# Gathered expert rows in a diffusion trunk: first gathers placed among the gate-matrix builds, selections reordered

## The chip, the core and the metric

The kernel runs on one core of a Trainium2 chip. The metric is the device time of one launch in microseconds (us). A profiled execution gives a trace; its span is the time from the first to the last instruction.

The engines: PE is TensorE (matrix multiplication), DVE is VectorE, ACT is ScalarE, POOL is GpSimd (here it issues the gathers), SP issues most other transfers. Each engine works through a queue of its own, in order.

## The reference

Two layers of a trunk; the part that matters here is the channel mixer of each layer, a lookup of single-neuron experts. 640 tokens (128 of a context, 512 of a sample) choose 8 x 16 of 16384 experts each.

```python
def peer_ffn(h, wq, k1, k2, u, v):
    q = (xt @ wq).reshape(n, PEER_HEADS, PEER_DKEY)
    s1 = jnp.einsum('thd,hnd->thn', q[..., :half], k1)
    s2 = jnp.einsum('thd,hnd->thn', q[..., half:], k2)
    v1, i1 = lax.top_k(s1, PEER_TOPK)
    v2, i2 = lax.top_k(s2, PEER_TOPK)
    cand = v1[..., :, None] + v2[..., None, :]
    cidx = i1[..., :, None] * PEER_NKEYS + i2[..., None, :]
    top, pos = lax.top_k(cand.reshape(...), PEER_TOPK)
    idx = jnp.take_along_axis(cidx.reshape(...), pos, axis=-1)
    g = jax.nn.softmax(top, axis=-1)
    ...
    act = jax.nn.gelu(jnp.einsum('td,thkd->thk', xc, u[ic]))
    w = gc * act
    return jnp.einsum('thk,thkd->td', w, v[ic])
```

## The kernel before

A layer is `mix` (projections, linear attention, convolution, neighbourhood attention) and then `peer`, which the change touches. `peer` splits the 640 tokens into five tiles of 128, numbered 0 to 4, and computes them in two ways.

**Tiles 0 and 1: gathered.** For each of 128 slots (8 heads x 16 experts) POOL fetches one row of `uv` per token, 128 x 2048 floats, 1 MB in one indirect transfer. `gather(t, s0)` does two slots, and `pump()` takes the next such pair from the list `todo`, 128 pairs in all for a layer: two gathers, two dot products with the token's activations on DVE (L754), a gelu on ACT (L756), a product with the gate (L757), and two accumulations on DVE (L763). `uv` has four buffers (`NUV`), two pumps' worth.

**Tiles 2 to 4: dense.** All 16384 experts are run through PE for these 384 tokens in 128 blocks of 128 experts, and a gate matrix that is zero for experts not chosen masks the result. `dense(b)` loads 512 KB of `uT` and 512 KB of `uv` on SP's queue into the four `raw` buffers, splits each into a high and a low part (ACT L836, DVE L837), runs 24 matmuls into `ps_a` (L857 to L859), a gelu (ACT L861), the product with the gate block `gres` (DVE L862), a split of that (L869, L870) and 18 matmuls into `acc` (L877). The loop over `b` calls one pump in each block, tied behind the gate product of the block before (`tc.issue_after`).

**The gate matrix.** `build(i)` makes the gate matrix for 16 dense tokens at a time, 24 builds in all, eight per tile: one-hot matrices of the two halves of the expert index (DVE L782, L784, from `ixT`), scaled by the gates (ACT L788, from `gT`), a matmul per token into `ps_g` (PE L791), and evictions by ACT (L793, L799) and DVE (L797) to `gres` and `sg`; `sg` then goes to HBM (`gsp`, L802) and comes back in dense, block group by block group (L846).

**Selections.** `level1` takes the best 16 of 128 keys for two heads of a tile. `select(t)` combines them for tile t: candidates, the best 16 of 50, softmax (Exp on ACT, L675), index lookup by masks (L702). For tiles 0 and 1 it ends in `gidx` (L715), for the others in `ixT` and `gT`. It is nearly all DVE. Tiles 1 to 4 pass `level1` while the queries are projected; tile 0 passes it in step `l0`.

**Order.** `select(2)` comes first, then the steps of `ORDER`: `b2` is the eight builds of tile 2, `s3` is `select(3)`, `l0` is `level1` of tile 0, and so on. `select(1)` stands in the dense loop at block `BSEL` = 16. A planner lays out every engine's queue when the program is built: of the instructions that it takes to be ready, the one earliest in the program goes first, so that later work fills gaps.

In layer 0 the builds also call `ada_steps` (`NADA` = 2 steps for 8 tokens): the modulation of the next layer, 256 KB loads of `w_ada` into `NWA` buffers and two matmuls each (L162). The same buffers serve the first modulation at the kernel's start.

**Memory.** `kp` is a pool that lives from the projection of the queries to the end of the builds and holds `kk` (keys), `qd` and others. The pools of dense (`raw`, `u`, `v`) open after it has closed, in its place.

Of the kernel before, what the change touches and what calls it, by code (L numbers as in the profile page):

```python
# [10 lines left out]
F32 = mybir.dt.float32  # L11
# [4 lines left out]
BF16 = mybir.dt.bfloat16  # L16
F16 = mybir.dt.float16
AF = mybir.ActivationFunctionType
OP = mybir.AluOpType
# [3 lines left out]
D = 1024  # L23
# [21 lines left out]
TD = T - TG  # L45
# [7 lines left out]
NUV = 4  # L53
# [6 lines left out]
ORDER = "b2 s3 b3 s4 l0 b4 s0".split()  # L60
BSEL = 16
ADA1 = 4
NWA = 4
# [6 lines left out]
class Trunk:  # L70
    def __init__(self, ctx, tc, I, O):
# [3 lines left out]
        V, S = self.V, self.S  # L75
# [16 lines left out]
        self.iota8 = consts.tile([128, 128, 8], BF16, name="iota8")  # L92
# [12 lines left out]
        V.tensor_copy(self.iota8, self.iota[:, :, None].to_broadcast([128, 128, 8]))  # L105
# [466 lines left out]
    def peer(self, l):  # L572
# [10 lines left out]
        ixT = gat.tile([128, 2, TD], BF16, name="ixT")  # L583
        gT = gat.tile([128, TD], F32, name="gT")
# [8 lines left out]
        kp = self.pool(f2, f"tk{l}", 1)  # L593
        f1 = ExitStack()
# [15 lines left out]
        def level1(units):  # L610
            ps = psb.tile([128, 2, 2, 128], F32, name="ps_k", tag="k")
            s2 = kp.tile([128, 2, 2, 128], F32, name="s2", tag="s2", bufs=3)
# [123 lines left out]
        gres = gpool.tile([128, NR, NTC, GB, TC], F32, name="gres")  # L736
        bp = self.pool(f2, f"gb{l}", 2)
        self.wp = bp

        ga = {}  # L740

        def gather(t, s0, n=2):
            if s0 == 0:
                ga["acc"] = gat.tile([128, D], F32, name="gacc", tag="gacc", bufs=1)
                ga["dots"] = gat.tile([128, 128], F32, name="dots", tag="dots")
                ga["w"] = gat.tile([128, 128], F32, name="gw", tag="gw")
# [20 lines left out]
        todo = [(t, s) for t in range(2) for s in range(0, 128, 2)]  # L767

        def pump(n=1):
            for _ in range(n):  # L770
                if todo:
                    gather(*todo.pop(0))
# [3 lines left out]
        def build(tcn):  # L776
            sg = bp.tile([128, NSP, GB, TC], F32, name="sg", tag="sg")
            for t8 in range(0, TC, 8):
# [5 lines left out]
                V.tensor_tensor(ohq, ixT[:, 1, None, t0:t0 + 8].to_broadcast([128, 128, 8]), self.iota8, op=OP.is_equal)  # L784
# [15 lines left out]
                for _ in range(NADA):  # L800
                    next(ada, None)
            nc.sync.dma_start(gsp[:, :, tcn].rearrange("r p b t -> p r (b t)"), sg.rearrange("p r b t -> p r (b t)"))  # L802
# [11 lines left out]
        select(2)  # L814
# [6 lines left out]
        gb = self.pool(st, f"gu{l}", NUV, side="right")  # L821
# [69 lines left out]
        for b in range(128):  # L891
            dense(b)
            if b == BSEL:
                select(1)
            with tc.issue_after(gates[max(0, b - GLAG)]):
                while todo and left - len(todo) < left * (b + 1) / 128:
                    pump()
# [111 lines left out]
```

## Time and profile before

| | |
|---|---|
| median of three runs | 4156.69 us (4152.92 to 4169.66) |
| span of the profiled execution | 4144.4 us |
| PE busy in it | 3810.6 us (92%) |
| DVE busy | 3333.9 us (80%) |
| ACT busy | 1701.2 us (41%) |
| POOL busy | 757.7 us (18%) |
| moved by DMA | 1011.89 MB, mean 244 GB/s |
| build stretch, layer 0 and 1 | 708 to 958 us, 2723 to 2948 us |
| dense stretch, layer 0 and 1 | 968.6 to 2098 us, 2957 to 4090 us |

A build stretch is counted from the first one-hot to the last eviction, a dense stretch from the first gelu (layer 0) or just ahead of the first blocks (layer 1) to the last block. Busy shares are averages over stages that have different limits, so the stretches say more than the whole span. Matmuls overlap and their ends are modelled, so a busy PE is not a PE at its peak.

### The profile page before, as it was taken

The page shows a single profiled execution, that of the slowest core. Times are in us where ns is not written, and L with a number is a line of the kernel's source. Part 1 is how long each engine was busy: PE and PEld are TensorE (multiplying, and loading weights), DVE is VectorE, ACT ScalarE, POOL GpSimd, SP SyncE. Part 2 cuts the span into 40 slices and gives each one's busy share as a digit, 9 for nine tenths or more (in the row PEclk, how much of TensorE's full clock was granted, in tenths as well). Part 3 has the DMA queues.
Part 4 walks back from the last instruction along what each step waited for, and adds up shares of the span by engine and source line. Part 5 has one row for each costly group of instructions (what it writes and reads, how often), then busy time and mean ns, then how long its engine had stood idle before and what let it go on. Part 6 is the DMA issues. An engine that isn't in the chain of part 4 may idle for free.

```text
span 4144.4 us, 54329 instructions
## 1 busy us (share of the span) xinstructions
PE 3810.6 (92%) x19884; PEld 3204.7 (77%) x19884; DVE 3333.9 (80%) x6618; ACT 1701.2 (41%) x3268; POOL 757.7 (18%) x532
## 2 busy tenths in 40 slices
PE   7999997888999999999989999867799999999998
PEld 4896775557888888888878988745688888888886
DVE  4762359788999999999968633988799999999997
ACT  4423332884333333333354243368633333333333
POOL 0000000002333333333300000000133333333331
PEclk8999998998999999999999999978899999999999
DMA  4124232668999999999921221023599999999995
GB/s 161 33 61 128 74 110 68 186 202 291 382 367 387 373 377 375 377 376 379 375 90 33 62 69 57 26 68 113 205 355 383 375 375 372 377 377 377 381 375 213
DMA packets 302267, 1011.89 MB, mean 244 GB/s; under 512 B 28273, under 2 KB 116721, under 8 KB 236209
## 3 DMA queue, kind: packets, MB, share of 16 engines
q0 software_dynamic: 73728, 536.90, 33.5%
q1 hardware_dynamic: 210560, 425.45, 29.4%
q10 hardware_dynamic: 17712, 46.07, 2.8%
q8 instruction: 156, 2.56, 0.2%
q14 instruction: 111, 0.90, 0.1%
HBM read 960.49 MB, written 47.84 MB: 243 GB/s over the span
## 4 chain that ended last, share of the span: by engine, by line
issue 37%; PE 29%; POOL 13%; ACT 9%; DVE 7%; DMA 5%; POOLq 0%; ACTq 0%; DVEq 0%; SPq 0%
PE ps_pj L235 13%; POOL uv L751 13%; ACT qg L788 5%; DMA uv<-uv,gidx 4%; PE ps_ada L162 2%; PE ps_lv L363 2%; PE ps_g L791 2%; PE acc L877 1%; PE npo L529 1%; ACT sg L799 1%; PE ps_s L508 1%; PE ps_ms L187 1%; ACT nt L208 1%; PE po L421 1%; PE pt L524 1%
## 5 line engine op out<-in xcount | busy, mean ns | idle before, releaser
L751 POOL DMA_INDIRECT uv<-uv,gidx x512 | 750.5, 1466 | 3317.0 <-PE ps_g L791 1766.2
L754 DVE SCALAR_TENSOR_TENSOR uv<-uv,ht 128x1024 f32<-128x1024 f32 x512 | 624.2, 1221 | 116.2 <-DMA uv<-uv,gidx 115.4
L859 PE MATMUL ps_a<-hd,ulo 128*128 128x384 f32 x2048 | 695.2, 339 | 17.8 <-DVE ulo L837 17.8
L857 PE MATMUL ps_a<-hd,uhi 128*128 128x384 f32 x2048 | 700.7, 342 | 9.6 <-ACT uhi L836 9.6
L858 PE MATMUL ps_a<-hd,uhi 128*128 128x384 f32 x2048 | 694.0, 339 | 0.0
L763 DVE SCALAR_TENSOR_TENSOR gacc<-uv,gw,gacc 128x1024 f32<-128x1024 f32 x508 | 652.5, 1284 | 15.7
L877 PE MATMUL acc<-vhi,whi 128*128 128x512 f32 x1536 | 506.2, 411 | 67.1 <-ACT whi L869 66.4
L877 PE MATMUL acc<-vhi,wlo 128*128 128x512 f32 x1536 | 486.9, 398 | 2.0 <-DVE wlo L870 1.7
L836 ACT ACTIVATE vhi<-raw 128x1024 fp32r<-128x1024 f32 x256 | 271.6, 1061 | 511.7 <-PE acc L877 496.1
L877 PE MATMUL acc<-vlo,whi 128*128 128x512 f32 x1536 | 480.0, 394 | 0.0
L859 PEld LDWEIGHTS ps_a<-hd,ulo 128*128 128x128 f32 x2048 | 388.3, 190 | 24.9 <-DVE ulo L837 22.7
L857 PEld LDWEIGHTS ps_a<-hd,uhi 128*128 128x128 f32 x2048 | 387.8, 189 | 21.2 <-ACT uhi L836 10.8
L877 PEld LDWEIGHTS acc<-vhi,whi 128*128 128x128 f32 x1536 | 271.6, 189 | 160.4 <-ACT whi L869 113.1
L858 PEld LDWEIGHTS ps_a<-hd,uhi 128*128 128x128 f32 x2048 | 387.7, 189 | 10.0
L788 ACT ACTIVATE qg<-ohq,gT 128x128 f32<-128x128 bf16 x768 | 341.3, 533 | 59.5 <-DVE ohq L784 59.5
L791 PE MATMUL ps_g<-ohp,qg 128*128 128x128 f32 x1536 | 297.9, 338 | 69.5 <-ACT qg L788 68.9
L791 PEld LDWEIGHTS ps_g<-ohp,qg 128*128 128x128 f32 x1536 | 238.4, 221 | 151.9 <-ACT qg L788 116.0
L877 PEld LDWEIGHTS acc<-vhi,wlo 128*128 128x128 f32 x1536 | 282.1, 189 | 81.7 <-DVE wlo L870 24.9
L877 PEld LDWEIGHTS acc<-vlo,whi 128*128 128x128 f32 x1536 | 290.3, 189 | 65.7
L837 DVE TENSOR_TENSOR vlo<-raw,vhi 128x1024 fp32r<-128x1024 f32 x256 | 312.1, 1219 | 13.5 <-ACT vhi L836 13.3
L756 ACT ACTIVATE gw<-dots 128x2 f32<-128x2 f32 x256 | 52.1, 203 | 646.6 <-DVE uv L754 646.4
L837 DVE TENSOR_TENSOR ulo<-raw,uhi 128x1024 fp32r<-128x1024 f32 x256 | 312.8, 1222 | 0.0
(243 smaller groups left out, 6187.5 us busy)
## 6 DMA issues: line engine op xcount, KB each, us to landing
raw<-uT SPq DMA_DIRECT2D x256, 512.0 KB, 6.4
raw<-uv SPq DMA_DIRECT2D x256, 512.0 KB, 8.4
wada<-w_ada SPq DMA_DIRECT2D x192, 256.0 KB, 3.3
gsp<-sg SPq DMA_DIRECT2D x48, 896.0 KB, 5.0
gres<-gsp ACTq DMA_DIRECT2D x112, 384.0 KB, 14.5
wraw<-w_in SPq DMA_DIRECT2D x56, 512.0 KB, 3.6
wraw<-w_out SPq DMA_DIRECT2D x16, 512.0 KB, 3.6
wraw<-wq SPq DMA_DIRECT2D x16, 512.0 KB, 4.0
```

The lines of the kernel that those rows point to most:

```text
L235: self.PE.matmul(ps[j][:, :n], w[:, k, :], x[:, k, :], start=(k == 0 and i == 0), stop=(k == 7 and i == 2))
L751: G.indirect_dma_start(out=b, out_offset=None, in_=I["uv"], in_offset=bass.IndirectOffsetOnAxis(ap=gidx[t][:, s:s + 1], axis=0))
L754: V.scalar_tensor_tensor(b[:, :D], b[:, :D], 1.0, ht[t], op0=OP.mult, op1=OP.mult, accum_out=dots[:, s:s + 1])
L763: V.scalar_tensor_tensor(acc_, b[:, D:], w[:, s:s + 1], acc_, op0=OP.mult, op1=OP.add)
L788: S.activation(qg[:, t, :], ohq[:, :, t4 + t], AF.Copy, scale=gT[:, t0 + t4 + t:t0 + t4 + t + 1])
L791: PE.matmul(ps[:, t, :], qg[:, t, :], ohp[:, t4 + t, :], start=True, stop=True)
L836: S.activation(hi, raw, AF.Copy)
L837: V.tensor_tensor(lo, raw, hi.bitcast(F32), op=OP.subtract)
L857: PE.matmul(ps, uhi[:, ks], hd[0][:, k, :], start=(k == 0), stop=False)
L858: PE.matmul(ps, uhi[:, ks], hd[1][:, k, :], start=False, stop=False)
L859: PE.matmul(ps, ulo[:, ks], hd[0][:, k, :], start=False, stop=(k == 7))
L877: PE.matmul(acc[:, t, j, :], a[:, ts], x[:, j * 512:(j + 1) * 512], start=(b == 0 and i == 0), stop=(b == 127 and i == len(parts) - 1))
```

## The change

The first 12 pumps of each layer move from dense into the builds, one after every second build (`EARLY` = 2), and work on tile 1, whose selection moves ahead of the builds; `todo` runs tile 1 first. `select(0)` takes the place of `select(1)` in dense. Dense spreads the remaining 116 pumps over its 128 blocks. To have the memory, `NWA` goes from 4 to 3, `s2` from three buffers to two, the pools of the gathers open ahead of the builds, `ixT` and `gT` move into `kp`, and `iota8` is made once in each layer, not kept.

```diff
-ORDER = "b2 s3 b3 s4 l0 b4 s0".split()
+ORDER = "s2 s1 b2 s3 b3 s4 l0 b4".split()
+EARLY = 2
-NWA = 4
+NWA = 3
...
-        self.iota8 = consts.tile([128, 128, 8], BF16, name="iota8")
-        V.tensor_copy(self.iota8, self.iota[:, :, None].to_broadcast([128, 128, 8]))
...
-        ixT = gat.tile([128, 2, TD], BF16, name="ixT")
-        gT = gat.tile([128, TD], F32, name="gT")
...
         kp = self.pool(f2, f"tk{l}", 1)
+        ixT = kp.tile([128, 2, TD], BF16, name="ixT")
+        gT = kp.tile([128, TD], F32, name="gT")
...
-            s2 = kp.tile([128, 2, 2, 128], F32, name="s2", tag="s2", bufs=3)
+            s2 = kp.tile([128, 2, 2, 128], F32, name="s2", tag="s2", bufs=2)
...
+        gx = self.pool(st, f"gx{l}", side="right")
+        gb = self.pool(st, f"gu{l}", NUV, side="right")
         bp = self.pool(f2, f"gb{l}", 2)
+        iota8 = bp.tile([128, 128, 8], BF16, name="iota8", tag="iota8", bufs=1)
+        V.tensor_copy(iota8, self.iota[:, :, None].to_broadcast([128, 128, 8]))
...
-                ga["acc"] = gat.tile([128, D], F32, name="gacc", tag="gacc", bufs=1)
-                ga["dots"] = gat.tile([128, 128], F32, name="dots", tag="dots")
-                ga["w"] = gat.tile([128, 128], F32, name="gw", tag="gw")
+                ga["acc"] = gx.tile([128, D], F32, name="gacc", tag="gacc")
+                ga["dots"] = gx.tile([128, 128], F32, name="dots", tag="dots")
+                ga["w"] = gx.tile([128, 128], F32, name="gw", tag="gw")
...
-        todo = [(t, s) for t in range(2) for s in range(0, 128, 2)]
+        todo = [(t, s) for t in (1, 0) for s in range(0, 128, 2)]
...
+            if tcn % EARLY == EARLY - 1:
+                pump()
             nc.sync.dma_start(gsp[:, :, tcn].rearrange("r p b t -> p r (b t)"), sg.rearrange("p r b t -> p r (b t)"))
...
-        select(2)
         for c in ORDER:
...
-        gb = self.pool(st, f"gu{l}", NUV, side="right")
...
             if b == BSEL:
-                select(1)
+                select(0)
```

## Rows read from the trace of the kernel before

**Rows 1.** Windows: us; busy us PE, PEld, DVE, ACT, POOL; clock, DMA, GB/s.

```profile
708.00:958.00 250.00, 213.82 (x1022) 131.57 (x1022) 199.75 (x613) 211.92 (x567) 4.63 (x4) 0.88 0.62 190
...
968.60:2098.00 1129.40, 1090.10 (x5345) 957.40 (x5344) 1048.98 (x1414) 398.47 (x636) 372.93 (x258) 1.00 0.96 370
...
2723.00:2948.00 225.00, 174.10 (x782) 130.12 (x782) 188.20 (x568) 204.43 (x555) 2.82 (x3) 0.86 0.35 106
...
2957.00:4090.00 1133.00, 1084.91 (x5285) 952.95 (x5284) 1045.74 (x1414) 398.97 (x633) 371.57 (x252) 0.99 0.96 369
```

**Rows 2.** Windows, middle of layer 0's dense stretch.

```profile
1100.00:2000.00 900.00, 868.19 (x4251) 761.82 (x4250) 834.59 (x1122) 318.30 (x506) 299.93 (x202) 1.00 0.98 377
```

**Rows 3.** First row: the gelu's line, 1100 to 2000. Others: timeline (start, length).

```profile
L861 ACT ACTIVATE w<-ps_a x101: 468/492/496, 1103.2 to 1994.1; 128x384 f32<-128x384 f32 x101
...
2062.88 0.49 ACT L861 ACTIVATE w<-ps_a 128x384 f32<-128x384 f32 x1 [1.04 <-PE ps_a L859]
...
2071.35 0.49 ACT L861 ACTIVATE w<-ps_a 128x384 f32<-128x384 f32 x1 [1.04 <-PE ps_a L859]
```

**Rows 4.** Waits of DVE, 1100 to 2000: us in total, times, longest.

```profile
DVE uv L754 <- DMA uv<-uv,gidx: 46.5, 39, 3.0
```

**Rows 5.** DMA view, 1100 to 2000: slices; issues, KB, us to landing.

```profile
GB/s 389 376 357 376 392 368 343 400 376 369 406 359 362 406 363 371 399 376 355 401 370 375 374 388 353 374 390 371 364 402 363 358 404 366 370 402 368 374 397 372
...
raw<-uT SPq DMA_DIRECT2D x102, 512.0 KB, 6.5
...
raw<-uv SPq DMA_DIRECT2D x101, 512.0 KB, 8.6
...
gres<-gsp ACTq DMA_DIRECT2D x52, 384.0 KB, 14.9
...
uv<-uv,gidx POOLq DMA_INDIRECT x202, 10.0
```

**Rows 6.** Windows, the 25 us ahead of layer 0's first one-hot.

```profile
683.00:708.00 25.00, 0.87 (x3) 0.50 (x3) 25.00 (x136) 1.24 (x2) 0.00 (x0) 0.58 0.09 31
```

**Rows 7.** Lines, 1100 to 2000: a pump's groups: busy, mean ns | idle before.

```profile
L754 DVE SCALAR_TENSOR_TENSOR uv<-uv,ht 128x1024 f32<-128x1024 f32 x202 | 246.6, 1221 | 46.6 <-DMA uv<-uv,gidx 46.5
...
L763 DVE SCALAR_TENSOR_TENSOR gacc<-uv,gw,gacc 128x1024 f32<-128x1024 f32 x202 | 259.6, 1285 | 7.2
...
L756 ACT ACTIVATE gw<-dots 128x2 f32<-128x2 f32 x102 | 20.8, 204 | 266.9 <-DVE uv L754 266.9
```

**Rows 8.** Timeline of DVE, layer 1: the two masks of `select(1)`.

```profile
2950.06 2.29 DVE L702 TENSOR_TENSOR mk<-pf,thr 128x2048 f16<-128x2048 f16 x1
...
3098.34 2.27 DVE L702 TENSOR_TENSOR mk<-pf,thr 128x2048 f16<-128x2048 f16 x1
```

**Rows 9.** Timeline of ACT, first gelu of layer 1's dense stretch.

```profile
2965.05 1.28 ACT L861 ACT_TABLE_LOAD   x1
...
2966.34 0.49 ACT L861 ACTIVATE w<-ps_a 128x384 f32<-128x384 f32 x1
```

**Rows 10.** Windows, undisturbed builds of layer 1.

```profile
2815.00:2840.00 25.00, 20.87 (x96) 14.80 (x96) 20.40 (x35) 24.93 (x70) 0.00 (x0) 0.94 0.36 109
```

**Rows 11.** Timeline, layer 1: end of `l0`, first dense load, last `qg`, first split.

```profile
2864.29 1.13 PE L614 MATMUL ps_k<-kk,qd 128*128 128x256 f32 x4 [0.65 <-DVE i L621]
...
2865.45 0.52 SPq L830 DMA_DIRECT2D raw<-uT  x1
...
2945.22 0.94 ACT L788 ACTIVATE qg<-ohq,gT 128x128 f32<-128x128 bf16 x2
...
2949.67 1.04 ACT L836 ACTIVATE uhi<-raw 128x1024 fp32r<-128x1024 f32 x1
```

**Rows 12.** DMA view, layer 0's build stretch, 708 to 958: issues.

```profile
wada<-w_ada SPq DMA_DIRECT2D x76, 256.0 KB, 4.8
...
uv<-uv,gidx POOLq DMA_INDIRECT x4, 10.1
```

**Rows 13.** Timeline of SP's queue at the kernel's start.

```profile
41.55 17.85 SPq L153 DMA_DIRECT2D wada<-w_ada  x15
```

More of the change, by code (lines that the diff above doesn't have):

```diff
@@ L783, in build @@
                                 self.iota[:, None, :].to_broadcast([128, 8, 128]), op=OP.is_equal)
-                V.tensor_tensor(ohq, ixT[:, 1, None, t0:t0 + 8].to_broadcast([128, 128, 8]), self.iota8, op=OP.is_equal)
+                V.tensor_tensor(ohq, ixT[:, 1, None, t0:t0 + 8].to_broadcast([128, 128, 8]), iota8, op=OP.is_equal)
                 for t4 in range(0, 8, 4):
```

## Prediction

> **What bounds the kernel now.** I read the stretches first, then the pace of one dense block, then who waits in it, then the build stretch instruction by instruction. Each layer has two stretches that the change touches. In the build stretch (from the first one-hot of `build` to the last eviction) VectorE (DVE), ScalarE (ACT) and TensorE (PE) are all busy for roughly three quarters or more and the DMA engines are far from full: 62% in layer 0, 35% in layer 1 [rows 1]. In the dense stretch PE, DVE and the DMA engines are all above 90%, and the middle of it moves 377 GB/s at a DMA share of 0.98 [rows 1, 2].
>
> Which of the three is last in dense? 100 blocks take 1994.1 - 1103.2 = 890.9 us, 8.91 us each; two blocks near the end, where nothing is late, are 2071.35 - 2062.88 = 8.47 us apart [rows 3]. The difference over 101 blocks, 101 x 0.44 = 44 us, is almost the 46.5 us in which DVE waits for gathered rows to land [rows 4]. So a block costs PE 8.47 us, and gathers that land late add 0.44. Bytes agree: a block moves two gathers of 128 x 2048 x 4 B (2.10 MB), two 512 KB loads (1.05 MB) and 52/101 of a 384 KB `gres` load (0.20 MB), 3.35 MB [rows 5]; 3.35 / 8.91 us = 376 GB/s, the rate of the stretch [rows 2].
>
> The sum is made against the profiled execution, whose span is 4144.4 us; the median of the runs is 4156.7, 12.3 us above it, and I carry that offset over.
>
> **Dense, what is removed.** With `EARLY` = 2 each layer's 24 builds run 12 pumps, 24 gathers; 116 of 128 pumps stay in dense. A block then moves 116/128 x 2.10 + 1.25 = 3.15 MB, 8.36 us at 377 GB/s: just below PE's 8.47. DVE had 834.6 / 101 = 8.26 us of work in a block [rows 2]. A pump is two dot products and two accumulations, 2 x (1.22 + 1.285) = 5.0 us [rows 7]; its two tiny operations lie in the overlaps of the others. DVE falls by 12/128 x 5.0 = 0.47 us and gets the first tile's selection spread over it (22.5/128 = 0.18): 7.97. So PE becomes the bound, with DMA at 99% of what it reached. I take 8.50 us: 128 x 8.50 = 1088 against 1129 and 1133 us [rows 1]: **-41 and -45 us**. Ends: 8.47 (1084) and 8.65 (1107, two fifths of the lateness stays).
>
> **Selection of the second tile ahead of the builds.** A selection fills DVE for the whole 25 us before the first build, with ACT at 1.2 and PE at 0.9 us [rows 6]; about 2.5 us of it is already the next selection's start, so 22.5 us is one. Now `select(1)` stands before `b2`, and whatever is earlier in the program wins DVE. ACT and PE wait for a second selection, less the 2.5 us that overlap: **+20 us** per layer. Before, this work was hidden: the last selection ran into DVE's gaps, in layer 1 its two masks 148 us apart, the second deep in dense [rows 8]. After, `select(0)` is the one that fills gaps, and its index is first needed by dense pump 53, near block 57. So I price it at nothing, its cover being the gaps left beside 7.97 us in 8.50; without them up to 10 us.
>
> **Build stretch, what is added.** DVE in layer 1: 188.2 us, less `select(0)` (22.5) and the part of `select(1)` in it (about 6), plus 12 x 5.0 = 60: 220. Layer 0: 199.8 - 22.5 - 15 + 60 = 222. The two shares of `select(1)` are estimates from how far it had come at the stretch's end. ACT: 12 gelus of 0.20 us [rows 7], and table switches, since selections use Exp and pumps Gelu: before, a layer loads a table for the first selection and one for the first dense gelu; now gelus stand between the Exps of `s3` and `s4`, five loads of 1.28 us [rows 9]. That is 2.4 + 6.4 = 9 us on an engine that is 24.9 of 25 us busy where builds run undisturbed [rows 10]. In layer 1, 225 us with ACT 204.4 becomes 213 of ACT and 220 of DVE. If DVE reaches the 92 to 93% it has in dense, 220 / 0.92 = 239: **+14**. In layer 0 neither engine is full before (ACT 85%, DVE 80%, PE 86%); I add the 9 us of ACT and 2 for PE waiting on `w_ada`: **+11**. Ends: 0 in layer 0 and +9 in layer 1 (all else goes into idle time), and DVE at its old share, 222/0.80 = 278 and 220/0.836 = 263 (+28, +38). The waits that are added: ACT's gelu waits for DVE's dot products with `qg` scalings queued behind it, hence PE's `ps_g`; DVE's first operation of a pump waits for its gather with `ohp` and `ohq` behind it. The gathers themselves I cost at nothing: POOL does nothing else, the four `uv` buffers keep two pumps in flight, and in layer 0 four gathers issued during builds landed in 10.1 us [rows 12], half the 20 us between pumps.
>
> On the table switch the row shows the load ending at 2966.33 and the gelu starting at 2966.34, with no gap [rows 9]. The Trainium skill, "ScalarE: Activation LUTs", section "What ACT_TABLE_LOAD costs", adds a drain of about 1.38 us to every switch, 2.66 us in all; by that the five switches would be an estimated 13 us, not 6.4, and the sum 14 us longer over both layers. The trace does not agree, so the rows' 1.28 stays.
>
> **Dense start.** `ixT` and `gT` move to the head of pool `kp`, whose place the dense loads' `raw` buffers take when the pool closes. Before, `kk` stood there: the first `raw` load went out at 2865.45, just after the last matmul on `kk` ended [rows 11], 84 us ahead of need. Now it waits for the last `qg` that reads `gT` (2945.22 + 0.94), with the other loads behind it on SP's queue, and takes some 6.5 us to land [rows 5]; the first split was at 2949.67 [rows 11]. **+4 us** per layer (ends 2 and 6).
>
> **Start of the kernel.** `NWA` 4 to 3 also reaches the first modulation matrices, where SP issues 15 loads in 17.85 us, 1.19 us each, as buffers come free [rows 13]. Four buffers make that a turnaround of 4.8 us; with three, 1.6 us each if landing stays the same, 15 x 0.4 = 6 us; less if landings quicken. **+4 us**, once (0 to 6). In the builds of layer 0 the loads land in 4.8 us [rows 12] and two are asked for in each half build, 250/48 = 5.2 us; I left 2 us for it above. `iota8` (one more small DVE copy in all) and `s2` with two buffers (both its writer and readers are on DVE) cost nothing.
>
> **Sum.** Layer 0: 20 + 11 + 4 - 41 = -6. Layer 1: 20 + 14 + 4 - 45 = -7. With +4: -9, **4148 us**, which is no change: 0.5% (21 us) is about what can be told from none here.
>
> **Rivals.**
> - *The build stretch swallows the pumps.* DVE idles 50 us in layer 0's stretch and 37 in layer 1's [rows 1], about what 60 us less the departed selections ask. Then layer 0 stays at 250, layer 1 grows by ACT's 9, dense runs at 8.47 and the load wait costs 2: 20 + 0 + 2 - 45 = -23, 20 + 9 + 2 - 49 = -18, +2: **4118**. For: idle time is there. Against: much of it is DVE waiting for ACT and PE in an order fixed beforehand, and layer 1's ACT is nearly full.
> - *The build stretch becomes DVE-bound (slower).* The mechanism: DVE's queue is in order, a pump's operations stand between one-hots, and each hand-over to ACT's gelu and back idles both. Place: the build stretch; price: DVE at its old share, +28 and +38: 20 + 28 + 4 - 41 = 11, 20 + 38 + 4 - 45 = 17, +4: **4189**. It decides for slower once the stretches grow by over about 27 us on average.
> - *The DMA side stays the bound of dense.* If gathers and loads are served at only 357 GB/s, as in some slices [rows 5], a block needs 3.15 / 357 = 8.83 us, 1130 us: 36 and 35 us lost, +4: **4232**. Against: 377 over 900 us. The Trainium skill, "DMA: Bandwidth & Descriptors", section "Where 436 GB/s comes from", puts what one core gets from HBM at about 358 GB/s, which would make this the outcome; the trace differs, with 377 GB/s in the mean of the stretch [rows 2] and only single slices at or under 358 [rows 5].
> - *The change does not do what it says*: the planner puts the pumps' arithmetic behind the builds after all. Then dense is unchanged and the costs stay: 2 x 24 + 4 = +52, **4209**. Against: `l0`, earlier in the program than `b4`, ran ahead of its one-hots, and a pump's place is as plain.
>
> **How the numbers follow.** Forecast 0.36, swallowed 0.34, DVE-bound 0.20, not done 0.06, DMA 0.04. Faster by over 0.5% is the second, 0.34; within 0.5% the first, 0.36; slower the rest, 0.30. As faster and slower cases hold most of the chance, the forecast's own range is 4136 to 4177; the wide one runs from below the swallowed case (both layers at their low ends) to the not-done one, 4100 to 4209.
>
> **What would show it.** The first build 20 us later after the last level-1 operation in each layer; gathers on POOL from about the first build; five more table loads; a build stretch near 239 to 261 us with DVE above 85%; blocks 8.5 us apart and the wait of DVE on gathers nearly gone; DMA under 0.98 only in the blocks without a pump; the first dense load after the last `qg`. I am wrong if dense stays at 8.8 or if the build stretch moves by less than 5 or more than 27 us.

## The result: 4262 us, 2.5% slower

| | before | after |
|---|---|---|
| median | 4157.3 us (4152.9 to 4169.7) | 4261.6 us (4251.0 to 4269.2) |
| ratio, 95% interval | 1 | 1.0254 (1.0234 to 1.0273) |
| span of the profiled execution | 4144.4 us | 4249.2 us |

The forecast was 4148 us, the range 4100 to 4209. The change is slower, and by more than the range allowed. (The median before is here that of four runs; the section on the time before had three of them.)

The windows of the kernel after, in the columns of [rows 1]: build stretch and dense stretch of layer 0, then of layer 1.

```profile
726.00:1038.40 312.40, 223.75 (x1022) 129.77 (x1022) 241.31 (x638) 219.59 (x583) 34.72 (x28) 0.84 0.69 227
1055.20:2168.70 1113.50, 1085.52 (x5348) 958.89 (x5346) 993.85 (x1337) 393.62 (x622) 335.58 (x236) 1.00 0.93 353
2803.50:3079.10 275.60, 181.37 (x782) 141.88 (x782) 237.12 (x625) 215.14 (x573) 35.06 (x26) 0.73 0.54 177
3093.50:4210.40 1116.90, 1088.16 (x5350) 961.60 (x5348) 997.78 (x1342) 393.78 (x623) 338.79 (x228) 0.99 0.93 353
```

From here on a build stretch runs from the first one-hot to the last eviction to `gres`, a dense stretch from its first gelu to its last. So the 104.8 us split up without a remainder:

| us | before | after | difference | predicted |
|---|---|---|---|---|
| first one-hot of layer 0 | 708.0 | 725.8 | +17.8 | +24 |
| build stretch, layer 0 | 248.6 | 312.6 | +64.0 | +11 |
| to the first dense gelu | 12.0 | 16.8 | +4.8 | +4 |
| dense, layer 0 | 1128.2 | 1113.5 | -14.7 | -41 |
| to the first one-hot of layer 1 | 626.2 | 634.8 | +8.6 | +20 |
| build stretch, layer 1 | 224.2 | 275.6 | +51.4 | +14 |
| to the first dense gelu | 19.2 | 14.3 | -4.9 | +4 |
| dense, layer 1 | 1139.2 | 1116.9 | -22.3 | -45 |
| end | 38.9 | 38.8 | 0 | 0 |

Two terms carry the miss: the builds cost 115 us instead of 25, and dense gave 37 us instead of 86. What stood ahead of the builds came out cheaper than forecast.

In the middle of the build stretch there is something that no window of the kernel before shows. Windows of 25 us in layer 0 and layer 1 of the kernel after:

```profile
827.00:852.00 25.00, 0.00 (x0) 0.00 (x0) 24.57 (x41) 0.61 (x3) 5.97 (x5) 0.52 0.65 239
2880.00:2905.00 25.00, 0.90 (x4) 0.60 (x4) 25.00 (x55) 4.75 (x10) 7.20 (x6) 0.56 0.56 191
```

PE and ACT do next to nothing for 25 us while DVE is full: tile 2's builds are over, and tile 3's cannot begin, since `select(3)` is not done. PE's wait says the same (waits of PE over layer 1's build stretch: total, times, longest):

```profile
PE pt L719 <- DVE f L716: 32.8, 1, 32.8
```

And in dense DVE still waits for gathered rows, 25.3 us in 900 where [rows 4] had 46.5 (waits of DVE, 1200 to 2100, kernel after):

```profile
DVE uv L757 <- DMA uv<-uv,gidx: 25.3, 20, 3.0
```

### The profile page after: what moved, and what is told of

It reads as the page before. It is cut to its first block, busy times and chain, and to the rows that moved or that the text cites. A ratio compares the mean times of both kernels' runs of the same rounds, so it can differ in the third digit from the quotient of the medians.

```text
span 4249.2 us, 54342 instructions
## 1 busy us (share of the span) xinstructions
PE 3814.6 (90%) x19884; PEld 3212.3 (76%) x19884; DVE 3336.1 (79%) x6619; ACT 1713.7 (40%) x3280; POOL 750.8 (18%) x532
## 4 chain that ended last, share of the span: by engine, by line
issue 40%; PE 29%; POOL 11%; DVE 8%; ACT 6%; DMA 6%; POOLq 0%; ACTq 0%; DVEq 0%; SPq 0%
PE ps_pj L234 13%; POOL uv L754 11%; DMA uv<-uv,gidx 4%; ACT qg L791 3%; PE ps_ada L161 2%; PE ps_lv L362 2%; PE ps_g L794 2%; PE acc L880 2%; DMA wada<-w_ada 2%; PE npo L528 1%; PE ps_ms L186 1%; PE ps_s L507 1%; ACT sg L802 1%; ACT nt L207 1%; PE pt L523 1%
## 5 line engine op out<-in xcount | busy, mean ns | idle before, releaser
L860 PE MATMUL ps_a<-hd,uhi 128*128 128x384 f32 x2048 | 697.9, 341 | 17.3 <-ACT uhi L839 16.6
L862 PEld LDWEIGHTS ps_a<-hd,ulo 128*128 128x128 f32 x2048 | 386.0, 188 | 16.9 <-DVE ulo L840 15.1
L794 PEld LDWEIGHTS ps_g<-ohp,qg 128*128 128x128 f32 x1536 | 247.0, 230 | 186.1 <-ACT qg L791 147.1
L880 PEld LDWEIGHTS acc<-vhi,whi 128*128 128x128 f32 x1536 | 271.4, 189 | 131.8 <-ACT whi L872 87.2
L880 PEld LDWEIGHTS acc<-vhi,wlo 128*128 128x128 f32 x1536 | 285.7, 189 | 72.0 <-DVE wlo L873 11.5
L234 PE MATMUL ps_pj<-hhi,whi 128*128 128x320 f32 x896 | 287.4, 324 | 19.6 <-ACT hhi L210 10.7
```

Source lines behind the costliest of these rows:

```text
L234: self.PE.matmul(ps[j][:, :n], w[:, k, :], x[:, k, :], start=(k == 0 and i == 0), stop=(k == 7 and i == 2))
L794: PE.matmul(ps[:, t, :], qg[:, t, :], ohp[:, t4 + t, :], start=True, stop=True)
L860: PE.matmul(ps, uhi[:, ks], hd[0][:, k, :], start=(k == 0), stop=False)
L862: PE.matmul(ps, ulo[:, ks], hd[0][:, k, :], start=False, stop=(k == 7))
L880: PE.matmul(acc[:, t, j, :], a[:, ts], x[:, j * 512:(j + 1) * 512], start=(b == 0 and i == 0), stop=(b == 127 and i == len(parts) - 1))
```

## The experiments

Two questions: why do twelve pumps cost the builds so much, and why does taking them out give dense so little? Each ratio is to the kernel before, measured beside it. An edit is to the changed kernel where nothing else is said; lines left out are marked with dots. All stretches stand in one table at the end of this section.

### Which part of the change costs the time

**No pumps in the builds.** It leaves the order of selections, the memory and `NWA`.

```diff
-EARLY = 2
+EARLY = 99
```

> The changed kernel with no pump in the builds (EARLY = 99, all 128 pumps in dense); the new order of selections, the memory and NWA = 3 stay. Theory A (pumps among the builds lengthen the build stretches, 312 and 274.6 us, by delaying the selection chain on VectorE): the stretches fall back to about 250 and 225 us, dense is as before the change, and the time is that of before plus the start (6), the query stage (3), the earlier selections (2 x 9) and the dense starts (2 x 4): about 4192 us. Rival B (memory: three w_ada buffers): layer 0's stretch stays at 280 to 300 us, layer 1's falls: about 4230. Rival C (the order of selections itself): both stretches stay above 265 us: about 4250.

Measured: 4193.9 us, 1.0087 (1.0070 to 1.0103). Stretches 253.2 and 236.7 us. The pumps in the builds therefore cost 59 and 39 us of the 64 and 51; order and memory cost the other 5 and 12, and 16 and 8 us ahead of the builds. Theory A gave the total, but only its first half is tested here: that the pumps do it, not how.

**Four `w_ada` buffers in the changed kernel, and three in the kernel before.** The edit of the changed kernel; in the kernel before it is the other way round.

```diff
-NWA = 3
+NWA = 4
```

> The changed kernel with four w_ada buffers instead of three. Theory B (layer 0's extra 64 us come from TensorE waiting for w_ada, 63 us of waits against 5 before): layer 0's build stretch falls by 30 to 50 us to 262 to 282, the start by 6: about 4215 us. Theory A (delayed selection chain): only the start falls, layer 0's stretch stays within 8 us of 312: about 4253. Layer 1 unchanged in both (274.6 within 4).

> The kernel before with three w_ada buffers instead of four and nothing else changed. If three buffers alone starve layer 0's builds: start +6, build stretch 250 to 280 or more, total about 4190. If they do so only together with the gathers: start +6, stretch within 5 us of 250, total about 4163 to 4167.

Measured: 4250.0 us, 1.0228 (1.0211 to 1.0245), with the first one-hot 5.9 us earlier and stretches of 312.0 and 275.2 us; and 4160.5 us, 1.0014 (1.0001 to 1.0027), first one-hot 6.8 us later, stretches 245.3 and 226.2. The third buffer's loss costs the start 6 to 7 us and the builds nothing. Theory B falls.

**Pumps held behind their own builds.** `last` is the last eviction to `gres`.

```diff
             if tcn % EARLY == EARLY - 1:
-                pump()
+                with tc.issue_after(last.ins):
+                    pump()
```

> The changed kernel with each early pump held back by the planner until the last eviction to gres of its own build is placed, so that the pumps of tile 3's builds can no longer fill VectorE while tile 3's selection runs. Theory A (pumps pulled ahead delay that selection, which leaves the 25 and 32 us in which TensorE has nothing): the holes shrink to under 8 us, stretches about 285 and 243, total about 4205 us. Rival D (the pumps' work and hand-overs simply fill VectorE, wherever they stand): stretches within 10 us of 312 and 274.6, total 4245 to 4265.

Measured: 4271.1 us, 1.0282 (1.0265 to 1.0299); stretches 317.4 and 278.4. Theory A falls in this form: with tile 3's pumps held back, PE still waits 24.9 us at one place in layer 1 and 18.8 in layer 0, where under 8 were expected. But the stretch moved inside. In layer 1 tile 2's builds became 7.6 us shorter and tile 3's 10.4 us longer, as the pumps went from one to the other. That led to a new theory, which cuts the build stretch by tiles.

### The build stretch is three phases

Tile 3's first build needs `select(3)`, tile 4's needs `select(4)`. So each tile's eight builds are a phase that ends no sooner than the DVE work placed in it. Windows from the first one-hot of a tile to that of the next (to the last eviction for tile 4), layer 1, tiles 2, 3 and 4. Kernel before:

```profile
2723.00:2793.50 70.50, 57.31 (x257) 43.43 (x257) 59.08 (x172) 67.60 (x183) 0.00 (x0) 0.84 0.31 92
2793.50:2875.40 81.90, 59.41 (x271) 43.51 (x269) 67.97 (x199) 68.63 (x187) 0.00 (x0) 0.87 0.41 127
2875.40:2947.10 71.70, 57.38 (x256) 43.18 (x256) 60.25 (x191) 67.72 (x185) 1.95 (x3) 0.86 0.31 93
```

The changed kernel without pumps in the builds (`e1_no_early`):

```profile
2766.30:2845.70 79.40, 58.52 (x259) 45.92 (x259) 68.03 (x197) 68.59 (x185) 4.37 (x4) 0.80 0.46 146
2845.70:2930.70 85.00, 59.81 (x267) 45.60 (x267) 71.20 (x231) 68.42 (x185) 0.00 (x0) 0.80 0.29 87
2930.70:3003.00 72.30, 59.00 (x256) 47.00 (x256) 56.28 (x140) 68.27 (x185) 0.00 (x0) 0.76 0.30 90
```

The kernel after, layer 0's three and then layer 1's:

```profile
725.80:854.20 128.40, 78.14 (x355) 43.58 (x355) 100.70 (x217) 76.31 (x200) 23.04 (x18) 0.81 0.75 255
854.20:953.20 99.00, 77.97 (x363) 43.59 (x363) 78.42 (x276) 71.89 (x190) 3.02 (x3) 0.88 0.64 201
953.20:1038.40 85.20, 67.65 (x304) 42.59 (x304) 62.38 (x148) 71.40 (x193) 8.66 (x8) 0.86 0.67 216
2803.50:2915.60 112.10, 60.47 (x259) 48.60 (x259) 99.65 (x214) 74.23 (x196) 24.61 (x18) 0.67 0.64 217
2915.60:3005.00 89.40, 62.80 (x267) 48.22 (x267) 76.84 (x270) 69.94 (x186) 2.19 (x3) 0.75 0.40 129
3005.00:3079.10 74.10, 58.10 (x256) 45.06 (x256) 60.63 (x144) 70.96 (x191) 8.26 (x6) 0.80 0.55 175
```

The reader is to hold the second column (the length) against the fifth (DVE). In layer 1's phases here a phase is 11 to 14 us longer than DVE's work in it wherever that is above some 58 us; ACT's 68 us give a floor of 70 to 72. Pumps raise tile 2's DVE from 68.0 to 99.7 us (+31.6) and its length from 79.4 to 112.1 (+32.7). They raise tile 3's by 5.6 and 4.4 and tile 4's by 4.4 and 1.8.

So the idle time of DVE that the average showed was not room for pumps. In layer 1 it was 36.8 us before, in all three phases alike (11.4, 13.9 and 11.5); it is 41.2 without pumps and 38.5 with them. Most of it is DVE waiting for ACT and PE within the builds, nearly as much after as before (waits of DVE over layer 1's build stretch, before, then after):

```profile
DVE ohq L784 <- ACT qg L788: 14.9, 29, 1.8
DVE sg L797 <- ACT gres L793: 12.7, 22, 1.1
DVE ohp L782 <- PE ps_g L791: 8.2, 17, 1.5
```
```profile
DVE ohp L785 <- PE ps_g L794: 13.7, 18, 1.7
DVE ohq L787 <- ACT qg L791: 11.8, 18, 1.7
DVE sg L800 <- ACT gres L796: 6.9, 13, 1.1
```

Only tile 4, where ACT is the fuller engine, takes in a little, 4.4 us of DVE work for 1.8 us of length. The prediction had divided the DVE work of the whole stretch by a share, as if the idle time would shrink; and the planner had put half of the pumps in tile 2, beside `select(3)` and the rest of `select(1)`.

**All twelve pumps in tile 4's builds.**

```diff
-            if tcn % EARLY == EARLY - 1:
-                pump()
+            if tcn >= 16:
+                pump(1 + tcn % 2)
```

> The changed kernel with all 12 early pumps in the eight builds of tile 4, one and two in turn, none in the builds of tiles 2 and 3. Theory P (each tile's builds are a phase of its own, as long as the fuller of VectorE and ScalarE in it; a pump costs the phase 5.0 us of VectorE once VectorE is the fuller): tiles 2 and 3 return to what they take without pumps (90 and 88 us in layer 0, 79 and 85 in layer 1), tile 4 has 35.5 + 17 (26.5) + 60 = 112 (122) us of VectorE work; stretches about 290 and 286 us, total about 4250. Rival H (the loss is the hole at the hand-over between tiles, which delayed selections make; with no selection left behind the pumps they fill idle time): tile 4 stays at ScalarE's 81 to 90 us, stretches about 265 and 252, total about 4195.

Measured: 4238.6 us, 1.0188 (1.0170 to 1.0206); stretches 285.7 and 262.5, between the two theories. Tiles 2 and 3 are back at 91 and 88 us (layer 0), 79 and 85 (layer 1), as theory P says. Tile 4 of layer 1:

```profile
2958.20:3056.80 98.60, 62.15 (x256) 54.11 (x256) 84.45 (x120) 72.88 (x196) 27.02 (x20) 0.60 0.81 279
```

DVE 84.5 and length 98.6, again 14 apart (28 in layer 0, where `w_ada` is loaded too). The rule holds, with no selection waiting behind; my 112 to 122 us had counted work in tile 4 that ran in tile 3 or in dense. Rival H had tile 4 at ACT's 81 to 90 us, which 98.6 and 106.6 pass; its 252 us for layer 1's stretch is nearer to the 262.5 than theory P's 286, so that the next run decides.

**A pump after every build.**

```diff
-EARLY = 2
+EARLY = 1
```

> The changed kernel with a pump after every build (EARLY = 1): 24 in the builds, 104 in dense. Theory P: the 12 more pumps of a layer cost 5 us each in the phases that are full of VectorE work and less in tile 4's: 40 to 60 us per layer on top of 312 and 276; dense gains as much again as the first twelve gave against none (27 and 20 us), or less as it nears its floor of 8.44 x 127 = 1072; total 4285 to 4335. Rival H (a hole per hand-over, whatever the number of pumps): under 20 us more per layer, total at or below 4262.

Measured: 4338.5 us, 1.0442 (1.0426 to 1.0458); stretches 385.5 and 324.6. In layer 1 the phases are 132.8, 108.8 and 83.0 us with 119.0, 95.3 and 70.9 us of DVE work: 12 to 14 us apart. Twelve more pumps cost 73 and 49 us, and bring dense 18 and 23. Rival H, with under 20 us more, falls. In layer 0 the phases are 34, 38 and 27 us longer than DVE's work, more than with twelve pumps.

**Four pumps where DVE has room, and the old place for the selection.**

```diff
-ORDER = "s2 s1 b2 s3 b3 s4 l0 b4".split()
+ORDER = "s2 b2 s3 b3 s4 s1 l0 b4".split()
-NWA = 3
+NWA = 4
...
-            if tcn % EARLY == EARLY - 1:
+            if tcn > 16 and tcn % EARLY == EARLY - 1:
```

> A version meant to pay: the changed kernel with four w_ada buffers, the order s2 b2 s3 b3 s4 s1 l0 b4 (the second tile's selection behind the first two tiles' builds again) and only four early pumps, all in tile 4's builds, where VectorE has 52 to 62 us of work in 72 to 75. Theory P: start as before the change, first build as before, tiles 2 and 3 at 84 and 85 us (layer 0), 71 and 82 (layer 1), tile 4 with 35.5 + 18 + 20 = 74 us of VectorE work beside 80 of ScalarE: stretches 250 and 228; dense with 124 pumps gains 4 x 2 us a layer: total 4140 to 4155, the kernel before or a little under. Rival H: any pump among builds opens hand-over holes: 4170 or more.

Measured: 4182.7 us, 1.0061 (1.0046 to 1.0076). The four pumps cost tile 4 little: it takes 77.4 and 74.0 us (79.7 and 71.7 before). But `select(1)` now fills tile 3, as its window in layer 1 shows:

```profile
2823.50:2924.10 100.60, 61.49 (x271) 43.87 (x269) 88.93 (x298) 68.64 (x189) 3.77 (x4) 0.81 0.38 124
```

88.9 us of DVE work, 100.6 us long: 12 apart again. And dense with 124 pumps ran 1139.9 and 1139.7 us, no faster than with 128. The expectation missed both; the total lies where rival H had put it (4170 or more), by the selection in tile 3 and not by holes in tile 4.

### Arithmetic or transfers

Layer 0's phases with pumps are 21 to 28 us longer than DVE's work, those of the kernel before 15 to 18. Layer 0 also loads `w_ada` in the builds. Three kernels split the early pumps; in their edits `math` is false, or `early` true, for the pumps in the builds alone.

**Transfers alone.** The early gathers are issued, their arithmetic is left out.

```diff
...
                 uv.append(b)
+                if not math:
+                    continue
...
+            if not math:
+                if s0 == 0:
+                    V.memset(acc_, 0.0)
+                return
```

> The changed kernel whose 12 early pumps per layer issue their 24 gathers but leave out all arithmetic on them (dot products, gelu, gate, accumulation; the sum starts at zero instead). Theory P (VectorE's work in a phase): the stretches are those without pumps, 253 and 237 us within 5, and dense is that of the changed kernel (1113 and 1117). Rival T (the gathers' traffic and the start of their transfers slow the builds, by w_ada or gsp): layer 0's stretch stays above 270 us, layer 1's above 245.

Measured: 4273.6 us, 1.0275 (1.0259 to 1.0292); stretches 312.7 and 287.9. At first sight that clears DVE. But nothing paced the gathers: POOL issued all 24 in one run, one every 2.7 us once the buffers were full. All the loss lies in tile 2 (133.0 us in layer 1; 84.0 and 70.9 for the others, as without pumps), where a write of `sg` stood behind them (waits of DVE, 2803 to 3079):

```profile
DVE sg L806 <- DMA gsp<-sg: 54.0, 2, 29.6
```

So this kernel shows another illness than the changed one, in whose layer 1 no wait of that kind is above 0.5 us. Two kernels that keep the pace better separate the halves.

**Arithmetic alone.** The early pumps' dot products and sums take the other tile's activations; nothing is fetched.

```diff
-                G.indirect_dma_start(out=b, out_offset=None, in_=I["uv"],
-                                     in_offset=bass.IndirectOffsetOnAxis(ap=gidx[t][:, s:s + 1], axis=0))
+                if not early:
+                    G.indirect_dma_start(out=b, out_offset=None, in_=I["uv"],
+                                         in_offset=bass.IndirectOffsetOnAxis(ap=gidx[t][:, s:s + 1], axis=0))
                 uv.append(b)
-                V.scalar_tensor_tensor(b[:, :D], b[:, :D], 1.0, ht[t], op0=OP.mult, op1=OP.mult,
+                V.scalar_tensor_tensor(b[:, :D], ht[1 - t] if early else b[:, :D], 1.0, ht[t], op0=OP.mult, op1=OP.mult,
...
+                bv = ht[1 - t] if early else b[:, D:]
```

> The changed kernel whose 12 early pumps per layer do all their arithmetic at their places but fetch nothing: the dot products and the sums take the other tile's activations instead of gathered rows, and the 24 early gathers of a layer are left out. Phase theory (a tile's builds last as long as VectorE's work in them plus 12 to 14 us in layer 1, 15 to 17 in layer 0, wherever that is over ScalarE's 68 to 72): layer 1 keeps its 112, 89 and 74 us (stretch 272 to 278), layer 0 takes 116, 94 and 80 (285 to 295), the 20 us to 312 being the transfers' beside w_ada. Rival T (the gathers' landing is the cost): stretches fall to 253 to 262 and 237 to 245.

**Paced transfers alone.**

```diff
...
                 uv.append(b)
+                if early:
+                    V.tensor_copy(dots[:, s:s + 1], b[:, 0:1])
+                    continue
...
+            if early:
+                if s0 == 0:
+                    V.memset(acc_, 0.0)
+                return
```

> The complement: the 12 early pumps per layer fetch their 24 rows, each read by one VectorE operation of a single column at the place of its dot product, so that the gathers keep some pace; dot products, gelu, gate and accumulation are left out (the sum starts at zero). Phase theory: layer 1 as without pumps, 237 within 6; layer 0 253 plus up to 25 for w_ada loads that land late, 265 to 280. Rival T: layer 1 above 255, layer 0 above 290.

Measured: 4238.4 us, 1.0201 (1.0177 to 1.0224), stretches 296.4 and 271.4; and 4219.2 us, 1.0146 (1.0121 to 1.0170), stretches 296.8 and 251.4.

| build stretch, us | layer 0 | layer 1 |
|---|---|---|
| no pump in the builds | 253.2 | 236.7 |
| arithmetic alone | 296.4 (+43) | 271.4 (+35) |
| paced transfers alone | 296.8 (+44) | 251.4 (+15) |
| both, the kernel after | 312.6 (+59) | 275.6 (+39) |

In layer 1 the arithmetic alone makes nine tenths of the cost: the phase theory holds there. With arithmetic alone, layer 0's tiles 2 and 3 are 16 us longer than DVE's 101.2 and 79.4, as without pumps, so the further 5 to 12 us in the kernel after go with the transfers. The transfers alone cost more than I expected in both layers; in layer 0 they came out as rival T had it (above 290). Their pace is only roughly that of the changed kernel, since DVE, with less to do, reads the rows sooner, so I take +44 and +15 as upper bounds, which no run tests. For layer 1 the trace supports it: with transfers alone DVE waits there for writes of `sg` to land, which the kernel after does for 0.5 us (waits of DVE, 2795.7 to 3047.1, `e10_paced_transfers`):

```profile
DVE sg L807 <- DMA gsp<-sg: 17.4, 2, 9.9
```

In layer 0 each half alone costs nearly as much as the other, and how the 59 us divide stays open between them. What the transfers hurt there is `w_ada` (waits of PE over layer 0's build stretch: no pumps, arithmetic alone, paced transfers, kernel after):

```profile
PE ps_ada L161 <- DMA wada<-w_ada: 10.3, 12, 3.8
```
```profile
PE ps_ada L161 <- DMA wada<-w_ada: 11.9, 13, 5.8
```
```profile
PE ps_ada L161 <- DMA wada<-w_ada: 48.6, 14, 13.9
```
```profile
PE ps_ada L161 <- DMA wada<-w_ada: 26.8, 13, 4.6
```

Some 10 us of the wait are there without early gathers, in the kernels with three buffers; the rest comes with the gathers, and a fourth buffer left 21.7 us of it (`e2_nwa4`).

### What holds dense back

| lateness in dense: length less 127 x 8.44 us | layer 0 | layer 1 |
|---|---|---|
| before, 128 pumps | 56 | 67 |
| no pump in the builds, 128 pumps | 69 | 65 |
| after, 116 pumps | 42 | 45 |
| a pump after every build, 104 pumps | 23 | 22 |

8.44 us is what most blocks take in the kernels with four or five buffers (the median block takes 8.42 to 8.46). Two executions of programs that are alike in dense differ by up to 11 us (the kernel before with four and with three `w_ada` buffers: 1128.2 and 1138.8 us in layer 0), so single differences are rough. Means over like kernels: 128 pumps 1138 us, 116 pumps 1117, 104 pumps 1095, that is 1.8 us per pump (`e4_b4_pumps`, where one or two of the twelve ran on into dense, lies between with 1128). The prediction took 41 and 45 us for twelve, 3.4 to 3.8 each. What POOL waits for in the kernel before gives a candidate (1100 to 2000):

```profile
POOL uv L751 <- DVE gacc L763: 559.3, 101, 8.4
```

Once in each block, POOL waits for a buffer that an accumulation frees. The loop of one buffer, from the timelines of POOL and DVE (kernel before):

```profile
1505.63 0.93 POOL L751 DMA_INDIRECT uv<-uv,gidx  x1 [0.30 <-issue]
...
1514.05 0.94 POOL L751 DMA_INDIRECT uv<-uv,gidx  x1 [0.30 <-issue]
```
```profile
1507.85 1.22 DVE L754 SCALAR_TENSOR_TENSOR uv<-uv,ht 128x1024 f32<-128x1024 f32 x1
...
1510.33 2.61 DVE L763 SCALAR_TENSOR_TENSOR gacc<-uv,gw,gacc 128x1024 f32<-128x1024 f32 x2
...
1517.17 1.23 DVE L754 SCALAR_TENSOR_TENSOR uv<-uv,ht 128x1024 f32<-128x1024 f32 x1 [0.77 <-DMA uv<-uv,gidx]
```

From the dot product at 1507.85 to the end of the accumulations at 1512.94 the arithmetic holds a buffer for 5.1 us; the next gather into it goes out 1.1 us later, at 1514.05. With four buffers a buffer has two blocks for its round, 16.9 us, so the rows must land within 16.9 - 5.1 - 1.1 = 10.7 us of their issue. The median is 10.0 [rows 5]; the gather issued at 1505.63 took 11.5 and made DVE wait. By this estimate the depth of the queue sets the limit, not the bytes.

**Five buffers and three, in the kernel before.** For the room of the fifth, `iota8` is made per layer and `ixT` and `gT` stand in `kp`, as in the changed kernel, where DVE still waits for rows in dense; three buffers (`NUV = 3`) need no room.

```diff
-NUV = 4
+NUV = 5
```

> The kernel before with five buffers for gathered rows instead of four (room from iota8 made per layer and ixT and gT in kp, as in the changed kernel). It asks what holds a block of dense back by 1.9 us per pump. Theory Q (the depth of the gather queue: a gather cannot start before an old buffer is free): dense falls from 1128 and 1139 us to about 1095 to 1110 in each layer, total 4100 to 4135. Rival R (the rate at which rows land, whatever the depth): dense within 8 us of before, total 4150 to 4170 with the later dense start.

> The kernel before with three gather buffers instead of four. Theory Q: a gather waits longer for a free buffer, so lateness grows by as much or more than the 55 us per layer that the fifth buffer removed: dense 1190 us or more in each layer, total above 4270. Rival R: the same bytes at the same rate, total within 30 us of 4157.

Measured with five: 4057.6 us, **0.9757 (0.9733 to 0.9781)**, dense 1077.0 and 1080.3 us with all 128 pumps. Window and wait of DVE, 1100 to 2000:

```profile
1100.00:2000.00 900.00, 898.56 (x4470) 801.56 (x4469) 875.53 (x1177) 331.68 (x533) 300.63 (x214) 1.00 1.00 395
```
```profile
DVE uv L754 <- DMA uv<-uv,gidx: 0.2, 1, 0.2
```

Measured with three: 4568.8 us, 1.1003 (1.0984 to 1.1021), dense 1317.7 and 1340.9 us (1200 to 2100):

```profile
1200.00:2100.00 900.00, 772.04 (x3603) 674.45 (x3602) 708.84 (x951) 268.55 (x429) 207.45 (x171) 0.94 0.87 319
```
```profile
DVE uv L754 <- DMA uv<-uv,gidx: 147.3, 94, 4.7
```

The same rows in the same number: 319, 377 and 395 GB/s with three, four and five buffers. Theory Q holds, and five buffers gave more than the 1095 to 1110 us expected. Against [rows 2], the row of five buffers has PE at 898.6 of 900 us and DVE at 875.5; the 0.98 of the DMA engines there was no ceiling.

**Five buffers in the dense stretch of the changed kernel.** The builds keep their four. `ixT` and `gT` also move behind `qd` in `kp`, by the edit that the next experiment shows.

```diff
-        gb = self.pool(st, f"gu{l}", NUV, side="right")
+        g4 = ExitStack()
+        gb = self.pool(g4, f"gu{l}", NUV, side="right")
...
         f2.close()
+        g4.close()
+        gb = self.pool(st, f"gv{l}", NUV + 1, side="right")
```

> The changed kernel with its four gather buffers during the builds and five in dense, ixT and gT behind qd. Theory Q (queue depth limits dense): dense falls from 1113 and 1117 us to 1075 to 1085 in each layer, the builds keep 312 and 276, total 4180 to 4200, 130 us or more above the kernel before with five buffers: the early pumps then bring dense nothing. Rival R (bytes or VectorE's work limit it): dense of 116 pumps comes out 20 us or more below the 1077 and 1080 that five buffers gave with 128 pumps, or does not fall.

Measured: 4192.3 us, 1.0098 (1.0083 to 1.0114); stretches 307.8 and 275.8, dense 1082.0 and 1089.5. With the fifth buffer, 116 pumps take dense no less time than 128 (1077 and 1080), so moving pumps out of dense brings nothing there, and the change as a whole costs 135 us against `e11_before_nuv5` (a part of that is its order and memory, which cost 39 us in `e1_no_early`).

**`ixT` and `gT` behind `qd`, against `e11_before_nuv5`.** It aims at the dense start, which took 25 and 26 us from the last eviction in `e11_before_nuv5`.

```diff
         kp = self.pool(f2, f"tk{l}", 1)
-        ixT = kp.tile([128, 2, TD], BF16, name="ixT")
-        gT = kp.tile([128, TD], F32, name="gT")
...
         qd = kp.tile([128, PH, 128], F32, name="qd")
+        ixT = kp.tile([128, 2, TD], BF16, name="ixT")
+        gT = kp.tile([128, TD], F32, name="gT")
```

> The kernel before with five gather buffers, ixT and gT standing behind qd in pool kp instead of at its head, so that the first dense loads of raw do not wait for the last reader of gT. If the place of ixT and gT makes the late dense start (25 and 26 us from the last eviction to gres to the first gelu, against 12 and 19 in the kernel before), it falls to 10 to 20 us, total 4035 to 4052. If not (the start is late for another reason), the time stays at 4057 within 6.

Measured: 4053.7 us, **0.9761 (0.9748 to 0.9774)**; the start still takes 23.7 and 25.3 us. The place is not the cause. ACT waits 17.3 us there for one load of `uv`; why it lands so late stays open. This kernel and `e11_before_nuv5` are the fastest of the study, about 100 us under the kernel before and 205 under the changed one.

All stretches, in us:

| kernel | builds, layers 0 and 1 | dense, layers 0 and 1 | median |
|---|---|---|---|
| before | 248.6, 224.2 | 1128.2, 1139.2 | 4157 |
| after | 312.6, 275.6 | 1113.5, 1116.9 | 4262 |
| e1_no_early | 253.2, 236.7 | 1140.9, 1136.4 | 4194 |
| e2_nwa4 | 312.0, 275.2 | 1116.9, 1117.2 | 4250 |
| e3_before_nwa3 | 245.3, 226.2 | 1138.8, 1145.7 | 4161 |
| e4_b4_pumps | 285.7, 262.5 | 1130.5, 1125.7 | 4239 |
| e5_held | 317.4, 278.4 | 1115.6, 1123.1 | 4271 |
| e6_transfers_only | 312.7, 287.9 | 1116.2, 1125.3 | 4274 |
| e7_every_build | 385.5, 324.6 | 1095.1, 1094.2 | 4339 |
| e8_slack | 256.4, 244.4 | 1139.9, 1139.7 | 4183 |
| e9_arithmetic_only | 296.4, 271.4 | 1121.1, 1117.9 | 4238 |
| e10_paced_transfers | 296.8, 251.4 | 1124.3, 1120.1 | 4219 |
| e11_before_nuv5 | 244.2, 223.4 | 1077.0, 1080.3 | 4058 |
| e12_before_nuv3 | 244.5, 224.4 | 1317.7, 1340.9 | 4569 |
| e13_nuv5_late | 245.3, 223.0 | 1075.8, 1078.8 | 4054 |
| e14_after_nuv5 | 307.8, 275.8 | 1082.0, 1089.5 | 4192 |

## Why the prediction was wrong, point by point

**Build stretch, +11 and +14: wrong by 53 and 37 us.** Three steps failed. In layer 1 the DVE work makes 17 of the 37 us and the share 20.
- *The DVE work.* Forecast 222 and 220 us, measured 241 and 237. The pumps themselves were right at 5.0 us, and ACT's 213 in layer 1 was right (215). But I took `select(1)` out of the stretch and put it whole ahead of it. It ran ahead only for some 8 to 11 us, and the rest of it went on in tile 2's gaps. And `select(0)`, which I took out whole, ran in part in tile 4's builds (about 13 us of DVE work in layer 1, one of its two masks among it). The +20 for `select(1)` was right as a price and wrong in its place: without pumps, the new order costs layer 1 8 us ahead of the builds and 12 in them.
- *The share of 92 to 93%*, borrowed from dense. DVE had 84% in layer 1's builds before and has 86% after. It was the idle time in us that stayed, 36.8 before and 38.5 after, where 220 us in 239 left it 19; kept in us it gives 237 + 37 = 274 for the 275.6. In layer 0 I gave DVE's added work no price at all, as no engine was full; it cost its full time there, and the idle time grew as well, from 50 to 71 us (53 with the arithmetic alone).
- *Where the idle time lies.* A tile's builds wait for its selection, so two regimes follow each other, and they stood side by side in [rows 10] and [rows 6]: ACT full where builds run, DVE full where a selection is awaited. DVE idles in the first, for ACT and PE; a pump placed ahead of a selection lengthens the second. I used the first row for ACT's price and the second only for the start.

**The gathers in the builds at nothing: wrong.** I argued from four gathers that landed in 10.1 us [rows 12] that they would be in time. So they were: DVE waited 4.6 us for them in layer 0. But I did not ask what lands late because of them: `w_ada`, for which PE waited 26.8 us, against 0.5 before and 10.3 in the same order without early pumps. The 2 us put down for that were for the third buffer's loss, which alone costs the stretch nothing (`e3_before_nwa3`).

**Dense, -41 and -45: the step that failed is the limit.** I compared bytes with the 377 GB/s of [rows 2], found them 1% under PE's time and took the lateness for gone. The floor was right (five buffers: 1077 / 127 = 8.48 us a block), and so was reading [rows 4] as the lateness. The cause was not: 395 GB/s are to be had, and what made rows late was the round of four buffers. Twelve pumps fewer give the loop a free block after about every tenth, no more, and 42 and 45 us of lateness stayed. Even the end of 8.65 us (1107) was too low.

**Selection fills gaps in dense at nothing.** No run separates it. `select(0)` in dense with 128 pumps (`e1_no_early`) is 13 us longer in layer 0 and 3 shorter in layer 1 than the kernel before, about what two executions differ by.

**Start +4, dense start +4.** The start was 6 to 7 us, the upper end. The dense start came out at +4.8 and -4.9 us.

**Table loads.** Six in layer 1's build stretch instead of five, 1.28 us each, 7.7 us in all (lines of ACT, 2803 to 3079, kernel after; then the timeline at one of them):

```profile
L759 ACT ACT_TABLE_LOAD x3 | 3.8, 1283 | 0.1
L674 ACT ACT_TABLE_LOAD x3 | 3.8, 1283 | 0.1
```
```profile
2842.26 0.54 ACT L802 ACTIVATE sg<-ps_g 128x448 f32<-128x448 f32 x1
2842.82 1.28 ACT L759 ACT_TABLE_LOAD   x1
2844.11 0.20 ACT L759 ACTIVATE gw<-dots 128x2 f32<-128x2 f32 x1
```

The step was right but for one load. The drain that the Trainium skill, "ScalarE: Activation LUTs", section "What ACT_TABLE_LOAD costs", adds shows on neither side of the load: 0.02 us ahead of it, 0.01 behind.

**The rivals.** *DVE-bound* named the mechanism and the sign, in-order DVE work that the idle share does not absorb. Its price failed: +28 and +38, with my DVE sums, where 64 and 51 came. With the measured sums, and the old shares of 80% and 83.6%, it would have said 241/0.80 = 301 and 237/0.836 = 284, near the 312 and 276. *Swallowed* fell: the idle 50 and 37 us are not smaller with the pumps in (71 and 38.5). *The DMA side stays the bound* fell in its mechanism, though dense came near its 1130 us by chance: the Trainium skill's 358 GB/s ("DMA: Bandwidth & Descriptors", section "Where 436 GB/s comes from") is passed by 377 and by 395. *Does not do what it says* fell: gathers start with the index (750 us in layer 0), and eleven or twelve pumps ran in the builds.

## What to carry to other kernels

An engine's idle time in a stretch is not room by itself: look at what it waits for. Here DVE's 37 us in layer 1 were hand-overs within the builds, and 37 to 41 us stayed idle with no, twelve or twenty-four pumps added. Where stages wait for each other's results, put added work down at its full time in the stage that it enters. A DMA share of 0.98 is no proof that the bytes are the limit: look at what the issuing queue waits for, and add up the round of one buffer (issue, landing, use, release) against the time that its depth allows. Here one more buffer gave 2.4%, where moving the transfers lost 2.5%.

## What the runs showed of the hardware

- A DMA share of 0.98 at 377 GB/s still left 5%: with one more gather in flight the same kernel moved 395 GB/s, at a share of 1.00. What the share counts, no run here shows.
- Queued gathers delay other transfers strongly: with 24 of 1 MB issued in one run, a write of 896 KB held DVE up for 29.6 us (`e6_transfers_only`); without early gathers such waits came to 1.4 us in that stretch (`e1_no_early`).
- A gather's landing depends on what else is under way: median 10.0 us with four buffers [rows 5], 6.4 with three, where only 319 GB/s moved.
- PE's granted clock fell to 0.67 in the phase in which PE idled most (2803.5 to 2915.6), against 0.84 in that tile before. Within it, in the 25 us in which PE stood still, it was 0.56, near the lower of its two levels (1.2 of 2.4 GHz). Its busy time rose only from 57.3 to 60.5 us for nearly as many matmuls.
